# A mixture-of-experts kernel: four neighbouring weight rows to a partition, and tokens transposed by every fourth channel

## The chip, the core and the metric

The kernel runs on one core of a Trainium2 chip. The metric is the device time of one execution in microseconds (us). The engines of the core are TensorE (PE, with its weight loads shown apart as PEld), VectorE (DVE), ScalarE (ACT), GpSimd (POOL) and SyncE (SP, which here only issues transfers). Transfers run on 16 DMA engines.

## The reference

One layer of a decoder on 1024 tokens (and 16 learned ones) of 1024 channels: three mixers (a convolution, an attention with a forget gate, a state-space scan) that share one input projection, an output projection, and then a mixture of 16 experts, of which each token takes two. All data are float32. The part that the change touches:

```
    for e in range(N_EXPERTS):
        y = (jax.nn.silu(t @ w1[e]) * (t @ w3[e])) @ w2[e]
        out = out + gates[:, e:e + 1] * y.astype(jnp.float32)
```

`w1[e]` and `w3[e]` are 1024x256, `w2[e]` is 256x1024. The sum over 1024 channels in `t @ w1[e]` may be taken in any order, as long as both sides use the same one.

## The kernel before

The program has three stages: projections with convolution and scan (to about 300 us), attention and output projection with the router (to about 585 us), and the experts (585 us to the end). The first two are ordered by a scheduler with a timeline model; the experts run in an order written out by hand.

**One expert.** The router has left for each expert a list of its tokens in blocks of up to 128 (b = 0 and b = 1). POOL gathers a block by an indirect transfer (`gather`, L1210): tile `xg`, one token to a partition, 1024 channels and two gates along it. PE transposes it in two halves of 512 channels (`turn`, L1220): four transposes of 128x128 into one PSUM bank, so that channels lie on partitions. In a transpose the 128x128 piece of `xg` is the operand that PE loads (a row of PEld), and the identity matrix is streamed through. ACT copies a bank out as `xh` (L1226) and DVE writes the rest `xl` (L1227). PE multiplies by the weights with three products for each of the 8 channel blocks k (`mm3`, L280 to L282; high by high, high by low, low by high), the two matrices side by side as 512 columns. Both blocks of every expert are gathered and transposed; the products of b = 1 run only for experts with over 128 tokens. Then follow the gate (L1237 to L1240), two more transposes (L1246), the product with `w2`, a scaled copy out of PSUM (ACT L1466, or DVE L1464), and an indirect transfer that adds the rows to `h_d` in memory (`scatter`, L1263, POOL).

**Weights.** The weights of an expert come in three chunks of 1 MB: q = 0 and q = 1 hold 512 rows of `w1` and `w3` each, q = 2 is `w2`. Each has one of six buffers `eraw` (`raw_b`), 2048 words to a partition. SP issues the transfers (L1169, two for q < 2; L1173, one for q = 2). A chunk is split in two halves of 1024 words a partition (`split`, half a = 0 or 1): ACT rounds it to the high part (L1298), DVE takes the difference (L1299). As soon as half 1 of a chunk has been split, `refill` issues the next chunk of the list into the buffer that is free. Chunks of q < 2 are split at least half an expert ahead of their use.

**Before the change,** partition p takes for k = 0 to 3 the row q\*512 + k\*128 + p of `w1` and of `w3`: four runs of 1 KB each. In the buffer the four k follow one another, each with 256 words of `w1` and 256 of `w3`, so that half 0 of a chunk is k = 0 and 1 of both matrices. The transposes take 128 neighbouring channels each.

The order by hand (an expert's steps; a0, a1, b0, b1, w0, w1 are splits, t and x the transposes and their copies, f, g, u, v, s, e the products, gates and copies out):

```
ORDER = (
    "a0 f0 t00 t01 a1 ga f1 x00 s00 g0 t10 u0 x01 g1 w0 s01 v0 e00 e01 s1 x10 t11 w1 u1 b0 "
    "e10 b1 e11 x11 v1 "
).split()
```

Of the kernel before, what the change touches and what calls it, by code (L numbers as in the profile page):

```python
# [1147 lines left out]
def moe(nc, tc, p, out, dram, dr, A, bank, small, ident, mm3, rsqrt_steps, t_d, h_d, rt):  # L1148

    lst, sel, nbl = rt.lst, rt.sel, rt.nbl  # L1150
    V, S, G, PE, SY = nc.vector, nc.scalar, nc.gpsimd, nc.tensor, nc.sync
# [4 lines left out]
    raw_b = A.rot("eraw", [2048], 3, flex=False)  # L1156

    def v4(t):
        return t.rearrange("p (k f) -> p k f", k=4)

    def v2(t):
        return t.rearrange("p (k f) -> p k f", k=2)

    def load(e, q):

        raw = raw_b()
        if q < 2:
            for c, nm in ((0, "exp_w1"), (256, "exp_w3")):
                SY.dma_start(out=v4(raw)[:, :, c:c + 256],  # L1169
                             in_=p[nm][0, e, q * 512:q * 512 + 512, :].rearrange(  # L1170
                                 "(k p) f -> p k f", p=128))
        else:
            SY.dma_start(out=v2(raw), in_=p["exp_w2"][0, e].rearrange("(k p) f -> p k f", p=128))  # L1173
        return raw
# [6 lines left out]
    def load_raw(e, q):  # L1181
        return load(seq[e], q)
# [10 lines left out]
    for _ in range(3):  # L1193
        w = todo.pop(0)
# [12 lines left out]
    def gather(ix, xg=None):  # L1207
        xg = xg_b() if xg is None else xg

        G.indirect_dma_start(out=xg, out_offset=None, in_=t_d,  # L1210
                             in_offset=bass.IndirectOffsetOnAxis(ap=ix, axis=0),
                             bounds_check=NX - 1, oob_is_err=False)
        return xg

    def turn(xg, hf):

        tp = bank("xt").rearrange("p (k t) -> p k t", k=4)
        for k in range(4):
            c = (hf * 4 + k) * 128
            PE.transpose(tp[:, k, :], xg[:, c:c + 128], ident)  # L1220
        return tp

    def turned(tp, xx, hf):
# [57 lines left out]
    def shaped(t, q):  # L1281
        return v4(t) if q < 2 else v2(t)
# [51 lines left out]
    def come(b):  # L1334

        xx[0, b] = xh_b(), xl_b()
        for hf in range(2):
            turned(turn(xgs[0, b], hf), xx[0, b], hf)
        gs[0, b] = gate_of(xgs[0, b], picks(0, b))
# [87 lines left out]
    def do_turn(e, b, hf):  # L1427
        if not hf:
            xx[e, b] = xh_b(), xl_b()
        tps[e, b, hf] = turn(xgs[e, b], hf)  # L1430
# [90 lines left out]
    with tc.manual_schedule():  # L1521
# [3 lines left out]
        for e in range(NE):  # L1525
            at = e - late
            for w in ORDER + ["end"]:
                if w in steps:
                    f, d = steps[w]
# [36 lines left out]
    with tc.If(nmax > 2):  # L1566
        with tc.For_i(0, NE) as e:
            nb = nc.values_load(nbl[0:1, bass.ds(e, 1)], min_val=0, max_val=8)
            with tc.For_i(2, nb) as b:
                wt = []  # L1570
                for q in range(3):
                    raw, h, l = load(e, q), wh_b(), wl_b()
                    S.activation(out=h, in_=raw, func=AF.Copy)
                    V.tensor_tensor(out=l, in0=raw, in1=h.bitcast(F32), op=OP.subtract)
                    wt.append([shaped(h, q), shaped(l, q)])
                V.tensor_copy(out=ixd, in_=lst[:, bass.ds(e * 8 + b, 1)])
                V.tensor_copy(out=sld, in_=sel[:, bass.ds(e * 8 + b, 1), :]
                              .rearrange("p a b -> p (a b)"))
                xg, xx, yt = gather(ixd), (xh_b(), xl_b()), yt_b()
                for hf in range(2):  # L1580
                    turned(turn(xg, hf), xx, hf)
                g = gate_of(xg, sld)
                hp = bank("h")
                first(wt[:2], xx, hp)
                aa = gate_turned(turn_gate(gate(hp)))
                for hf in range(2):
                    yp = bank("y")
                    second(wt[2], aa, yp, hf)
                    V.tensor_scalar(out=yt[:, hf * 512:hf * 512 + 512], in0=yp, scalar1=g,
                                    scalar2=None, op0=OP.mult)  # L1590
                scatter(yt, ixd)
# [414 lines left out]
```

## Time and profile before

| | |
|---|---|
| time, median of 3 runs | 865.52 us (862.94 to 870.54) |
| profiled execution, its own time | 868.56 us |
| its span, first to last instruction | 866.9 us |
| PE busy | 788.9 us (91%) |
| PE weight loads busy | 641.0 us (74%) |
| DVE busy | 595.7 us (69%) |
| ACT busy | 433.9 us (50%) |
| POOL busy | 246.0 us (28%) |
| moved by DMA | 121.99 MB, 141 GB/s in the mean |

A group row of the profile reads: line, engine, operation, output <- inputs, partitions x elements, count | busy us, mean ns of one | idle time of the engine just before them and what ended it. A timeline row reads: start in us, length in us, engine, line, operation, count, and in brackets the idle time before it and who ended it. Matmuls overlap in the pipeline, so a row of eight lasts less than eight times one of them. The DMA share is the mean busy share of the 16 DMA engines.

### The profile page before, as it was taken

What the parts mean: (1) busy time and instruction counts of PE and PEld (TensorE: products, weight loads), DVE (VectorE), ACT (ScalarE), POOL (GpSimd) and SP (SyncE); (2) the same over time, 40 slices, a digit from 0 to 9 for tenths busy, and PEclk for the clock granted to TensorE, in tenths of its full rate; (3) what the DMA queues carried; (4) which work ended last, traced back from release to release, by engine and by line L of the source; (5) the groups of instructions that cost most, each with busy time, mean ns of one, the idle gap of its engine ahead of it and who ended that gap; (6) DMA issues with size and microseconds to landing.
All of it is one profiled execution on the core that took longest, in us unless ns stands there. A gap on an engine that the chain in (4) does not pass through costs nothing. (4 is left out here: it accounts for less than half of the span.)

```text
span 866.9 us, 13091 instructions
## 1 busy us (share of the span) xinstructions
PE 788.9 (91%) x4420; PEld 641.0 (74%) x4421; DVE 595.7 (69%) x1297; ACT 433.9 (50%) x785; POOL 246.0 (28%) x357
## 2 busy tenths in 40 slices
PE   3899899989999999999999999967999999897872
PEld 2899899969899965655657888855787787675662
DVE  6972599987754466666534336577788677887995
ACT  7222444524233256665564322144568565785861
POOL 4499766840001000000002010003224213323134
PEclk9998999979999999999999999988999999999996
DMA  9307131104310033021132335317699979979962
GB/s 279 84 7 140 33 104 44 43 19 117 100 53 21 13 112 133 25 74 59 64 121 55 122 122 170 122 74 241 197 292 288 276 230 271 305 248 273 326 262 107
DMA packets 89002, 121.99 MB, mean 141 GB/s; under 512 B 14843, under 2 KB 69914, under 8 KB 88928
## 3 DMA queue, kind: packets, MB, share of 16 engines
q1 hardware_dynamic: 81872, 101.98, 37.0%
q0 software_dynamic: 7056, 19.09, 8.2%
q8 instruction: 39, 0.64, 0.3%
q14 instruction: 35, 0.29, 0.1%
HBM read 101.16 MB, written 26.52 MB: 147 GB/s over the span
## 5 line engine op out<-in xcount | busy, mean ns | idle before, releaser
L280 PE MATMUL psum<-arena,arena 128*128 128x512 f32 (+4 forms) x848 | 306.3, 362 | 8.9 <-DVE arena L1461 2.4
L281 PE MATMUL psum<-arena,arena 128*128 128x512 f32 (+4 forms) x848 | 300.0, 354 | 2.0 <-DVE arena L341 2.0
L282 PE MATMUL psum<-arena,arena 128*128 128x512 f32 (+4 forms) x848 | 298.9, 353 | 0.0
L280 PEld LDWEIGHTS psum<-arena,arena 128*128 128x128 f32 x848 | 162.9, 193 | 29.9 <-issue 4.9
L281 PEld LDWEIGHTS psum<-arena,arena 128*128 128x128 f32 x848 | 163.4, 193 | 16.8 <-DVE arena L341 2.2
L282 PEld LDWEIGHTS psum<-arena,arena 128*128 128x128 f32 x848 | 162.8, 192 | 16.9 <-DVE arena L1227 0.4
L1299 DVE TENSOR_TENSOR arena<-arena,arena 128x1024 fp32r<-128x1024 f32 x96 | 113.5, 1220 | 12.6 <-ACT arena L1298 11.7
L1298 ACT ACTIVATE arena<-arena 128x1024 fp32r<-128x1024 f32 x96 | 98.6, 1071 | 0.0
L670 DVE CUSTOM_DVE_ANT_0 arena<-psum,arena 128x144 bf16<-128x144 f32 (+6 forms) x112 | 55.2, 507 | 47.5 <-PE psum L668 25.3
L725 ACT ACTIVATE arena<-psum,arena 128x512 f32<-128x512 f32 (+4 forms) x112 | 59.3, 539 | 47.9 <-PE psum L722 30.8
L728 PE MATMUL psum<-arena 128*65 128x512 f32 (+4 forms) x224 | 82.8, 455 | 0.5 <-ACT arena L725 0.5
L272 POOL TENSOR_SCALAR arena<-arena 128x1 f32<-128x1 f32 (+2 forms) x36 | 13.0, 361 | 246.9 <-ACT arena L845 72.1
L1263 POOL DMA_INDIRECT h_d<-arena x17 | 33.2, 1951 | 127.1 <-DVE arena L1227 38.9
L1226 ACT ACTIVATE arena<-psum 128x512 fp32r<-128x512 f32 x64 | 38.4, 603 | 28.4 <-PE psum L1220 28.4
L428 DVE SCALAR_TENSOR_TENSOR psum<-arena,psum 128x1024 f32<-128x1024 f32 x40 | 51.4, 1285 | 0.9
L1227 DVE TENSOR_TENSOR arena<-psum,arena 128x512 fp32r<-128x512 f32 x64 | 43.6, 684 | 12.1 <-ACT arena L1226 12.1
L665 PE MATMUL psum<-arena 128*128 128x144 f32 (+6 forms) x112 | 51.4, 483 | 0.0
L717 PE MATMUL psum<-arena 128*128 128x512 f32 (+4 forms) x112 | 47.8, 427 | 2.8 <-ACT arena L725 2.5
L438 POOL TENSOR_TENSOR arena<-arena 128x512 f32<-128x512 f32 x36 | 48.1, 1360 | 5.9 <-ACT arena L435 5.9
L1220 PE MATMUL psum<-arena 128*128 128x128 f32 x256 | 38.1, 283 | 11.8 <-DVE arena L1227 5.3
L435 ACT ACTIVATE arena<-arena 128x512 f32<-128x512 f32 x40 | 28.3, 721 | 38.0 <-POOL arena L438 24.8
L1220 PEld LDWEIGHTS psum<-arena 128*128 128x128 f32 x256 | 30.5, 144 | 22.6 <-issue 8.1
(299 smaller groups left out, 1250.6 us busy)
## 6 DMA issues: line engine op xcount, KB each, us to landing
arena<-in_exp_w_dram SPq DMA_DIRECT2D x64, 512.0 KB
arena<-in_exp_w_dram SPq DMA_DIRECT2D x16, 1024.0 KB
arena<-in_x_dram SPq DMA_DIRECT2D x16, 512.0 KB
arena<-in_w_in_dram SPq DMA_DIRECT2D x14, 512.0 KB
arena<-cr_d SPq DMA_DIRECT2D x8, 520.0 KB
arena<-in_w_out_dram SPq DMA_DIRECT2D x8, 512.0 KB
h_d<-arena SPq DMA_DIRECT2D x8, 512.0 KB
t_d<-arena SPq DMA_DIRECT2D x8, 512.0 KB
```

Of the source, the lines that this page charges most:

```text
L280: PE.matmul(out=acc, lhsT=lh[k], rhs=rh[k], start=(k == 0), stop=False)
L281: PE.matmul(out=acc, lhsT=lh[k], rhs=rl[k], start=False, stop=False)
L282: PE.matmul(out=acc, lhsT=ll[k], rhs=rh[k], start=False, stop=(k == n - 1))
L428: V.scalar_tensor_tensor(out=yc, in0=ub[:, m, w:w + NX], scalar=cwt[:, m, w:w + 1], in1=yc, op0=OP.mult, op1=OP.add)
L438: G.tensor_tensor(out=yp[:, a:a + 512], in0=yp[:, a:a + 512], in1=o, op=OP.add)
L665: PE.matmul(out=sp, lhsT=QS[:, i * 128 - 128:i * 128], rhs=KS[:, a:b], start=True, stop=not last)
L670: V.tensor_tensor_reduce(out=jk_b()[:, :b - a], in0=sp, in1=nrow[:, a:b], scale=1.0, scalar=-3.0e38, op0=OP.add, op1=OP.max, accum_out=mp[ ...
L725: S.activation(out=pt, in_=sp, func=AF.Exp, bias=ccol[:nk, j, h:h + 1])
L728: PE.matmul(out=po[:, q0 - 512 * g:512], lhsT=vt[:nk, j, h, :], rhs=pt, start=j == 0, stop=j == last, skip_group_check=True)
L1220: PE.transpose(tp[:, k, :], xg[:, c:c + 128], ident)
L1298: S.activation(out=h[:, cs], in_=raw[:, cs], func=AF.Copy)
L1299: eng.tensor_tensor(out=l[:, cs], in0=raw[:, cs], in1=h[:, cs].bitcast(F32), op=OP.subtract)
```

## The change

A partition now takes four neighbouring rows of `w1` (q\*512 + 4p to q\*512 + 4p + 3), which lie in memory as one run of 4 KB, and the same of `w3`. In the buffer the 1024 words of `w1` come first, then the 1024 of `w3`; half 0 of a chunk is `w1`, half 1 is `w3`. The moving operand of a product with block k is two runs of 256 words, 1024 words apart, where it was one run of 512. To match the new order of channels, a transpose takes every fourth channel of its half: 128 words, 16 bytes apart, where it took 128 neighbouring words. Numbers of instructions, sizes and the tiles' places are as before.

```
     def v4(t):
-        return t.rearrange("p (k f) -> p k f", k=4)
+        return t.rearrange("p (w k f) -> p k w f", w=2, k=4)
...
         if q < 2:
-            for c, nm in ((0, "exp_w1"), (256, "exp_w3")):
-                SY.dma_start(out=v4(raw)[:, :, c:c + 256],
+            for c, nm in ((0, "exp_w1"), (1024, "exp_w3")):
+                SY.dma_start(out=raw[:, c:c + 1024],
                              in_=p[nm][0, e, q * 512:q * 512 + 512, :].rearrange(
-                                 "(k p) f -> p k f", p=128))
+                                 "(p k) f -> p (k f)", p=128))
...
         for k in range(4):
-            c = (hf * 4 + k) * 128
-            PE.transpose(tp[:, k, :], xg[:, c:c + 128], ident)
+            PE.transpose(tp[:, k, :], xg[:, hf * 512 + k:hf * 512 + 512:4], ident)
         return tp
```

The first place where instructions stand otherwise is SP's list in the loop over experts, one expert's five weight transfers from its `w2` on; the branches are those of the conditional blocks (L1468 is the scatter's). Before (a wait on DVE is a wait for the split of the half that the transfer overwrites):

```order
L1173 DMA arena1_61<-in_exp_w2_dram 128x2x1024 [waits DMAHW3_49,DVE_49]
L1468 UNCONDITIONAL_BRANCH
L1169 DMA arena2_2796<-in_exp_w1_dram 128x4x256 [waits DMAHW4_49,DVE_49]
L1169 DMA arena2_2796<-in_exp_w3_dram 128x4x256 [waits DMAHW5_49]
L1169 DMA arena1_61<-in_exp_w1_dram 128x4x256 [waits DMAHW6_49,DVE_49]
L1169 DMA arena1_61<-in_exp_w3_dram 128x4x256 [waits DMAHW7_49]
```

And in the changed kernel:

```order
L1174 DMA arena1_61<-in_exp_w2_dram 128x2x1024 [waits DMAHW3_49,DVE_49]
L1170 DMA arena2_2796<-in_exp_w1_dram 128x1024 [waits DMAHW4_49,DVE_49]
L1468 UNCONDITIONAL_BRANCH
L1170 DMA arena2_2796<-in_exp_w3_dram 128x1024 [waits DMAHW5_49,DVE_49]
L1170 DMA arena1_61<-in_exp_w1_dram 128x1024 [waits DMAHW6_49,DVE_49]
L1170 DMA arena1_61<-in_exp_w3_dram 128x1024 [waits DMAHW7_49,DVE_49]
```

The transfer of `w1` waits for half 0 of its buffer alone and stands one branch earlier; that of `w3` has a wait of its own for half 1. On PE, DVE, ACT and POOL the order in the loop over experts is unchanged.

The second place is in the attention stage, where the scheduler's model of the shorter transfers has moved a split of the output projection's weights (L782) ahead of pieces of the row maxima (L670) on DVE; the same pieces of maxima (L665) stand later on PE:

```order
 L744 TENSOR_TENSOR arena_2795<-psum,arena_61 128x4x64
-L670 ISA arena_61<-psum,arena_61 128x328
-L670 ISA arena_61 128x1
-L670 ISA arena_61<-psum,arena_61 128x392
-L670 ISA arena_61 128x1
 L782 TENSOR_TENSOR arena_3626<-arena_2796,arena_3626 128x1024
```

Two pieces of the maxima that stood ahead of this split now stand behind it; what was computed there is computed all the same, a little later.

## Rows read from the trace of the kernel before

**Rows 1.** Busy time of the engines in five stretches of the expert stage (us).

```profile
core 0: us, PE busy (x) PEld busy (x) DVE busy (x) ACT busy (x) POOL busy (x), PEclk, DMA share, GB/s
592.00:712.00 120.00, 114.97 (x560) 92.75 (x559) 94.06 (x159) 80.43 (x126) 30.63 (x18) 0.97 0.82 256
712.00:745.00 33.00, 28.07 (x137) 21.15 (x136) 26.37 (x46) 23.20 (x38) 11.98 (x8) 1.00 0.98 287
745.00:785.00 40.00, 39.06 (x193) 31.23 (x192) 35.28 (x60) 29.83 (x47) 9.74 (x5) 1.00 0.86 271
785.00:801.00 16.00, 10.81 (x51) 7.89 (x50) 11.21 (x20) 10.77 (x17) 6.67 (x5) 1.00 0.96 277
801.00:836.00 35.00, 31.71 (x144) 24.32 (x144) 33.19 (x55) 26.25 (x46) 10.79 (x10) 0.95 0.84 300
```

**Rows 2.** The expert stage's weight splits and scaled copies on ACT, grouped by shape.

```profile
L1298 ACT ACTIVATE arena<-arena 128x1024 fp32r<-128x1024 f32 x91 | 93.7, 1072 | 0.0
L1466 ACT ACTIVATE arena<-psum,arena 128x512 f32<-128x512 f32 x39 | 26.9, 690 | 14.7 <-DMA h_d<-arena 14.7
```

**Rows 3.** Timelines of ACT and PE: the three places where a transfer is waited for longest.

```profile
721.02 0.69 ACT L1466 ACTIVATE arena<-psum,arena 128x512 f32<-128x512 f32 x1 [3.56 <-DMA h_d<-arena]
737.00 0.69 ACT L1466 ACTIVATE arena<-psum,arena 128x512 f32<-128x512 f32 x1 [4.42 <-DMA h_d<-arena]
795.94 0.69 ACT L1466 ACTIVATE arena<-psum,arena 128x512 f32<-128x512 f32 x1 [4.04 <-DMA h_d<-arena]
801.01 1.69 PE L1220 MATMUL psum<-arena 128*128 128x128 f32 x8 [4.78 <-DMA arena<-t_d,arena]
```

**Rows 4.** DMA traffic of 788 to 791.5 us, then of 832 to 836 us.

```profile
DMA packets 1348, 1.35 MB, mean 384 GB/s; under 512 B 34, under 2 KB 1348, under 8 KB 1348
...
DMA packets 466, 1.63 MB, mean 409 GB/s; under 512 B 67, under 2 KB 67, under 8 KB 466
```

**Rows 5.** Scatter: time to landing; and DMA queue 0 while one lands (703.4 to 713).

```profile
DMA to landing us min/median/max: 6.3/8.2/10.7
...
q0 software_dynamic: 144, 0.52, 27.6%
```

**Rows 6.** Grouped by shape, 586 us to the end: products, and loads for transposes.

```profile
L282 PE MATMUL psum<-arena,arena 128*128 128x512 f32 x264 | 105.7, 400 | 0.0
L1220 PEld LDWEIGHTS psum<-arena 128*128 128x128 f32 x256 | 30.5, 144 | 22.6 <-issue 8.1 <-DVE arena L1227 6.1 <-DVE arena L1252 2.8
```

**Rows 7.** Single lines: lengths min/median/max in ns; three on DVE, one on ACT.

```profile
L1935 DVE SCALAR_TENSOR_TENSOR arena<-arena x2: 1224/1225/1226, 205.5 to 212.3; 128x1024 f32<-128x1024 f32 x2
L1939 DVE SCALAR_TENSOR_TENSOR arena<-arena x2: 1187/1206/1225, 207.9 to 215.5; 128x1024 f32<-128x1024 f32 x2
L1948 DVE SCALAR_TENSOR_TENSOR arena<-arena x2: 2130/2148/2166, 216.6 to 231.0; 128x1024 f32<-128x1024 f32 x2
L1849 ACT ACTIVATE arena<-arena x1: 1920/1920/1920, 129.4 to 129.4; 128x2048 f32<-128x2048 f32 x1
```

**Rows 8.** Timeline of PE: eight transposes behind a product, and the product after them.

```profile
614.14 0.39 PE L282 MATMUL psum<-arena,arena 128*128 128x512 f32 x1
614.38 1.03 PE L1220 MATMUL psum<-arena 128*128 128x128 f32 x8
615.16 0.48 PE L280 MATMUL psum<-arena,arena 128*128 128x512 f32 x1
```

**Rows 9.** Timelines: transposes with two loaded columns; router products with 20 streamed columns.

```profile
388.32 0.60 PE L685 MATMUL psum<-arena 128*2 128x128 f32 x4 [0.23 <-ACT arena L686]
575.91 0.97 PEld L886 LDWEIGHTS psum<-arena 128*128 128x128 f32 x8 [0.98 <-ACT arena L883]
575.91 1.07 PE L886 MATMUL psum<-arena 128*128 128x20 f32 x8 [0.75 <-ACT arena L883]
```

**Rows 10.** The transposes in the same five stretches: PE busy, PEld busy, counts.

```profile
592.00:712.00 120.00, 19.76 (x135) 15.97 (x133) 0.97 0.82 256
712.00:745.00 33.00, 5.46 (x36) 4.01 (x36) 1.00 0.98 287
745.00:785.00 40.00, 5.87 (x43) 5.09 (x44) 1.00 0.86 271
785.00:801.00 16.00, 1.50 (x11) 0.97 (x10) 1.00 0.96 277
801.00:836.00 35.00, 5.23 (x32) 3.99 (x32) 0.95 0.84 300
```

**Rows 11.** Busy time of the engines in the attention stage, 430 to 460 us.

```profile
430.00:460.00 30.00, 29.77 (x152) 17.41 (x150) 10.35 (x30) 19.78 (x39) 0.75 (x2) 1.00 0.28 89
```

## The prediction

> **What bounds the kernel now.** The change lies in the expert stage, so I read the busy times by stretch first. From 592 to 712 us PE is busy for 114.97 of 120 us, and from 745 to 785 us for 39.06 of 40, while DVE and ACT have room [rows 1]: there, what PE is given in addition lengthens the kernel. In the other three stretches PE is idle for 4.9, 5.2 and 3.3 us. Next I ask whether weights are waited for, since the change makes their transfers shorter. They are not: ACT, which takes each chunk first, never sits idle ahead of its 91 splits [rows 2]. What ACT does wait for is the scatter of an earlier block, which must have left the buffer: 14.7 us in all [rows 2], and where it waits longest, at 721, 737 and 796 us, PE falls behind too; once PE itself waits 4.78 us for a gather [rows 3]. So transfers cost PE time at two places, 712 to 745 and 785 to 801 us, some 10 us together, through gather and scatter and not through the weights.
>
> **Weights' transfers.** Transfers of 1 KB runs alone ran at 384 GB/s, transfers of 4 KB rows (with rows from POOL's queue among them) at 409 GB/s [rows 4]. For the 2.1 MB of `w1` and `w3` of an expert that is 5.46 against 5.13 us, 0.33 us less, over 16 experts 5.3 us of DMA time. It is hidden as it is; it can only let gathers and scatters land earlier. Bounds: no gain at all, or all of the 10 us above. I take 2 us, near the lower end: a scatter needs 6.3 us to land at the least and 8.2 in the median [rows 5], and 0.33 us off each expert's traffic is small beside that.
>
> **Order of SP.** The transfer of `w1` waits for one half of its buffer instead of both, and passes a branch of SP. It starts earlier by about the time of one split (1.07 us on ACT [rows 2], a similar one on DVE). Nobody waits for it, so this gains nothing. Nothing waits longer either: that of `w3` gets the wait that both had. A first half of a chunk is now `w1` alone, so that the first product needs both halves; the splits of an expert's q < 2 chunks are done before its products start, so this is hidden.
>
> **The moving operand in two runs.** Each product reads 256 words, jumps, and reads 256 more. The trace of before has no such product. The nearest row is ACT's copy at L1849, which reads runs of 16 words and takes 1.92 us for 2048 elements, against 1.07 for 1024 in one run [rows 2, 7]: jumps at the end of such runs cost nothing. I take zero; each of three lines has 264 products, two thirds of them with `w1` and `w3` [rows 6], and if each of these 528 lost 0.01 us it would be 5 us.
>
> **The transposes.** This is the term that decides. A transpose loads 128 columns of `xg`; now they lie 16 bytes apart. What does a load cost? Eight transposes take 1.03 us; starts are 0.11 us apart [rows 8]. Two other rows say what sets these 0.11 us. Transposes with only two loaded columns and the same 128 streamed ones are 0.11 us apart too, (0.60 - 0.27)/3, so that the streaming alone takes that long [rows 9]. Products of the router with 128 loaded and only 20 streamed columns are also 0.11 us apart, (0.97 - 0.19)/7 [rows 9], so that the loading alone takes that long. (0.27 and 0.19 us are the lengths of the last one in the row.) Load and stream are level: a load lies exactly under the transpose before it, and a slower load shows in full.
>
> Would it be slower? The trace of before has no strided load of many columns. The nearest row for access in steps is on DVE: L1948 writes words 32 bytes apart and takes 2148 ns, where L1935 and L1939, the same operation on as many words in a row, take 1206 to 1225 [rows 7], a factor of 1.77. ACT's runs of 64 bytes are free, DVE's single words are not. [...] I take doubling, 0.22 us, near the factor of DVE and between the ends.
>
> [...]
>
> The sum: of four transposes behind a product, the first load has room under the product; three are longer by 0.11 us. That is 0.083 us a transpose. In the two stretches where PE is full there are 135 + 43 = 178 of them [rows 10]: 14.8 us. In the other three there are 79 [rows 10], 6.6 us; PE is idle there for 13.4 us in all, but its waits are not where the transposes are, so I count half, 3.3 us. Less 2 us for the transfers: 14.8 + 3.3 - 2 = **16.1 us slower**. The profiled execution took 868.56 us and would take 884.7. It lies 3.0 us above the median of the runs, 865.52; I forecast runs, so 865.5 + 16.1 = **881.6 us**.
>
> **The attention stage.** Maxima and a split change places. PE is busy there for 29.77 of 30 us and DVE for 10.35 [rows 11]; the same work is done by both, and PE has other products to fill in. I take zero; if PE once had to wait for the split that was put first, it would cost about that split's length, 1.2 us as for the like operations of DVE [rows 7].
>
> **Rivals.**
> - *The stepped load is as fast as before.* Then the transposes still start 0.11 us apart and what is left is the 2 us of the transfers: 863 to 866 us. [...] Against it: the factor of 1.77 on the only single-word row.
> - *Faster: gathers and scatters land early enough.* If loads are as fast as before and lighter traffic ends the waits of [rows 3], PE gains what it lost there, 4.9 + 5.2 = 10.1 us: 855.4 us. It decides where a scatter lands by some 4 us earlier than now, since that is how long ACT waits [rows 3]; against it, 0.33 us of traffic an expert is far from that.
> - *Longer packets hold up the scatter.* A scatter is 144 packets on the other queue, nine on each DMA engine [rows 5]. If an engine takes them in turn with SP's packets, each waits for 4 KB where it waited for 1 KB: at 409 GB/s over 16 engines [rows 4], 3 KB take 0.12 us, nine times 1.1 us. At the three places where ACT waits longest [rows 3] this is 3.3 us, and the kernel with fast loads and no other gain comes to 868.8 us: the 2 us are taken back and a little more. [...] No row here shows the turn.
> - *Still slower.* At DVE's 2.1 ns a word a load takes 0.27 us, 0.16 more than now; the same sum gives 0.118 us a transpose, 21.0 + 4.7 - 2 = 23.7 us, 889.2 us.
>
> **How the numbers follow.** Stepped loads slower (doubled, or up to DVE's rate): 0.50, with 872 to 892 as its own range (the lower end is a factor of 1.5 in place of 2, half of 18.1 us less 2 of gain, +7 us; the upper one the 889.2 us without all of the gain). Loads as fast, small effects of transfers in either direction, 860 to 869: 0.36. Loads as fast and the waits on transfers gone, 854 to 859: 0.14. The likeliest is the first, so the forecast is 881.6 us. The range reaches to 857 and 892: outside lie about half of the last case and 0.06 above. A measurement of this kernel tells apart about 1%. The first case is slower by over 1% in nearly all of its range, 0.47; its lowest part (0.03), and the second with 0.35, are within 1%; the third with its 0.14 and 0.01 of the second are faster, 0.15.
>
> **What would show it.** Eight transposes in a row: 1.03 us long now; over 1.6 us if loads double, the same if they don't, with the mean length of a load above its 144 ns [rows 6]. The rows between 592 and 712 us: PE stays full and the stretch with the same work gets longer. ACT's idle time ahead of L1466 tells which way the scatters went: under 14.7 us if transfers help, over it if the longer packets hold them up. A mean of the products above 400 ns [rows 6] would show the two runs of the moving operand. What would make it wrong: above all a stepped load that costs nothing.

## The result, and the profile after

The changed kernel takes 870.54 us in the median of 20 runs (865.91 to 874.24), the kernel before 866.45 us in 20 runs beside it, of which one, of 1530.23 us, was in a slow state and doesn't count. The medians lie 4.1 us apart; the ratio of the others is 1.0064, with a 95% interval of 1.0047 to 1.0081: slower by about 5.5 us (4.1 to 7.0), where 16.1 us were forecast (881.6 us). The range (857 to 892 us) holds it; "slower by over 1%" does not. The profiled execution took 868.15 us, its span is 866.5 us.

The page's busy times and SP's transfer queue, in the kernel after (engine, us, share, count; then queue, packets, MB, share of 16 engines):

```profile
PE 790.2 (91%) x4420; PEld 645.2 (74%) x4421; DVE 596.8 (69%) x1297; ACT 434.6 (50%) x785; POOL 248.0 (29%) x357
...
q1 hardware_dynamic: 57296, 101.98, 35.6%
```

PE is busy 1.3 us longer and its loads 4.2 us. SP's queue moved its 101.98 MB in 57,296 packets (81,872 before), and its share fell from 37.0% to 35.6%: the transfers did become lighter.

The spans of the two profiled executions hardly differ (866.9 and 866.5 us), and that misleads: before the expert stage, the granted clock fell in other places in the one than in the other (from 50 to 100 us it was 0.90 before and 1.00 after). So I take landmarks inside the expert stage. The program computes 32 gates on ACT (L1237). Here are all of them as a group, in the kernel before and then after (lengths in ns, first and last start in us), and after that the starts of four of them, before and after:

```profile
L1237 ACT ACTIVATE arena<-psum x32: 377/385/431, 602.1 to 834.7; 128x256 f32<-128x256 f32 x32
```

```profile
L1237 ACT ACTIVATE arena<-psum x32: 377/382/420, 595.6 to 834.3; 128x256 f32<-128x256 f32 x32
```

```profile
711.75 0.38 ACT L1237 ACTIVATE arena<-psum 128x256 f32<-128x256 f32 x1
742.22 0.41 ACT L1237 ACTIVATE arena<-psum 128x256 f32<-128x256 f32 x1
755.03 0.38 ACT L1237 ACTIVATE arena<-psum 128x256 f32<-128x256 f32 x1
815.31 0.38 ACT L1237 ACTIVATE arena<-psum 128x256 f32<-128x256 f32 x1
```

```profile
706.00 0.38 ACT L1237 ACTIVATE arena<-psum 128x256 f32<-128x256 f32 x1
739.73 0.38 ACT L1237 ACTIVATE arena<-psum 128x256 f32<-128x256 f32 x1
753.29 0.38 ACT L1237 ACTIVATE arena<-psum 128x256 f32<-128x256 f32 x1
814.98 0.38 ACT L1237 ACTIVATE arena<-psum 128x256 f32<-128x256 f32 x1
```

From the first gate to the last it is 232.6 us before and 238.7 us after. This **stretch of gates**, 6.1 us longer, is the measure that I use below for single profiles. By pieces, between the landmarks:

| piece | before | after | more |
|---|---|---|---|
| first gate to 711.75 (after: 706.00) | 109.6 | 110.4 | 0.8 |
| to 742.22 (739.73) | 30.5 | 33.7 | 3.3 |
| to 755.03 (753.29) | 12.8 | 13.6 | 0.7 |
| to 815.31 (814.98) | 60.3 | 61.7 | 1.4 |
| to the last gate | 19.4 | 19.3 | -0.1 |

In the first piece PE is full and over half of the transposes lie in it: it lost 0.8 us, where the forecast had 11. Over half of the loss lies in the second piece, where PE waits for transfers.

The rows that answer to [rows 1] (the same stretches), [rows 2] and [rows 6], in the kernel after:

```profile
592.00:712.00 120.00, 115.60 (x559) 95.20 (x559) 95.46 (x164) 81.79 (x129) 30.75 (x19) 0.97 0.75 252
712.00:745.00 33.00, 25.91 (x113) 20.00 (x112) 23.37 (x40) 19.07 (x32) 11.31 (x7) 0.90 0.92 265
785.00:801.00 16.00, 11.08 (x53) 8.66 (x51) 11.48 (x19) 9.65 (x14) 7.60 (x5) 0.92 0.88 263
```

```profile
L1466 ACT ACTIVATE arena<-psum,arena 128x512 f32<-128x512 f32 x39 | 27.0, 691 | 17.2 <-DMA h_d<-arena 17.2
L282 PE MATMUL psum<-arena,arena 128*128 128x512 f32 x264 | 106.8, 405 | 0.0
L1220 PEld LDWEIGHTS psum<-arena 128*128 128x128 f32 x256 | 38.7, 209 | 24.1 <-issue 15.3 <-DVE arena L1252 2.7 <-DVE arena L1227 2.6
```

ACT waits 17.2 us for scatters, where it waited 14.7. A load of a transpose takes 209 ns in the mean where it took 144. Of 712 to 745 us PE is busy for 25.91 us in place of 28.07, at a granted clock of 0.90 in place of 1.00. PE's two longest waits for gathers, there and at 794 us, and the row of eight transposes that answers to [rows 8]:

```profile
607.99 1.11 PE L1220 MATMUL psum<-arena 128*128 128x128 f32 x8
...
738.10 1.96 PE L1220 MATMUL psum<-arena 128*128 128x128 f32 x8 [4.57 <-DMA arena<-t_d,arena]
...
799.38 1.95 PE L1220 MATMUL psum<-arena 128*128 128x128 f32 x8 [4.74 <-DMA arena<-t_d,arena]
```

The second wait is that of [rows 3] (4.78 us before). The first is new: before, PE waited 0.41 us for this gather, and 1.57 us for DVE behind it. Eight transposes last 1.11 us in place of 1.03; the eight behind the wait last 1.96, at a granted clock of 0.50 (738.0 to 740.1 us). From 737 to 744 us, before and then after (columns as in [rows 1]):

```profile
737.00:744.00 7.00, 3.88 (x20) 2.34 (x18) 5.28 (x9) 7.00 (x12) 2.78 (x2) 1.00 0.98 293
```

```profile
737.00:744.00 7.00, 5.75 (x21) 4.72 (x21) 6.37 (x11) 3.60 (x6) 0.00 (x0) 0.51 1.03 306
```

After the wait of 4.57 us the granted clock is 0.51 of full speed in the mean of the 7 us; before, with PE idle for shorter pieces (0.41, 1.57, 0.48 and 0.66 us), it stayed at 1.00. A wait that long is not what it takes, though: in the kernel with the new buffer alone (below) PE waits 0.89 us for this gather and 1.46 us for DVE behind it, much as before, and the granted clock is 0.50 from 737 to 743.5 us.

Why does this gather come late? POOL's timeline at that place, before and then after (scatters L1263; the gather is L1210 before and L1211 after):

```profile
721.70 1.58 POOL L1263 DMA_INDIRECT h_d<-arena  x1 [4.80 <-ACT arena L1466]
728.63 1.56 POOL L1263 DMA_INDIRECT h_d<-arena  x1 [5.35 <-ACT arena L1298]
730.50 1.75 POOL L1210 DMA_INDIRECT arena<-t_d,arena  x1 [0.30 <-DVE arena L1240]
```

```profile
717.29 1.58 POOL L1263 DMA_INDIRECT h_d<-arena  x1 [3.42 <-ACT arena L1466]
726.22 2.12 POOL L1263 DMA_INDIRECT h_d<-arena  x1 [7.35 <-DMA h_d<-arena]
728.65 1.92 POOL L1211 DMA_INDIRECT arena<-t_d,arena  x1 [0.30 <-DVE arena L1227]
```

A scatter adds to `h_d`, so it waits on POOL until the one before it has landed, and the gather stands behind it. From the end of the issue of the first scatter to the gather's start it is 7.2 us before (730.50 - 723.28) and 9.8 us after (728.65 - 718.87). Before, the second scatter was released by ACT, so that the landing had come by then; after, the landing itself came last, 7.35 us behind the issue. What is late is the landing of the scatter. The DMA traffic while the packets of this scatter move, before (723.8 to 727.5 us) and then after (719.6 to 725.0 us):

```profile
DMA packets 265, 0.65 MB, mean 175 GB/s; under 512 B 15, under 2 KB 137, under 8 KB 265
...
q0 software_dynamic: 143, 0.52, 93.0%
q1 hardware_dynamic: 122, 0.12, 10.1%
```

```profile
DMA packets 411, 1.46 MB, mean 270 GB/s; under 512 B 58, under 2 KB 58, under 8 KB 410
...
q0 software_dynamic: 153, 0.50, 52.3%
q1 hardware_dynamic: 257, 0.94, 43.7%
```

The same scatter (queue 0) took 3.7 us while SP's queue (queue 1) moved 0.12 MB beside it, and 5.5 us with 0.94 MB beside it. Five scatters in the stage have 128 rows. From the trace's packets, first start to last end, they take 3.46, 4.15, 3.07, 3.68 and 3.57 us before, **3.59 us** in the mean, and 3.94, 5.99, 5.40, 5.46 and 5.17 us after, **5.19 us** in the mean. I call this mean the scatter's length below.

### The profile page after: what moved, and what is told of

The parts are those of the page before. It is cut to its first block, busy times and chain, and to the rows that moved or that the text cites. A ratio compares the mean times of both kernels' runs of the same rounds, so it can differ in the third digit from the quotient of the medians.

```text
span 866.5 us, 13118 instructions
## 1 busy us (share of the span) xinstructions
PE 790.2 (91%) x4420; PEld 645.2 (74%) x4421; DVE 596.8 (69%) x1297; ACT 434.6 (50%) x785; POOL 248.0 (29%) x357
## 3 DMA queue, kind: packets, MB, share of 16 engines
q1 hardware_dynamic: 57296, 101.98, 35.6%
## 5 line engine op out<-in xcount | busy, mean ns | idle before, releaser
L282 PE MATMUL psum<-arena,arena 128*128 128x512 f32 (+4 forms) x848 | 297.5, 352 | 0.0
L280 PEld LDWEIGHTS psum<-arena,arena 128*128 128x128 f32 x848 | 161.1, 190 | 28.7 <-issue 4.6
L281 PEld LDWEIGHTS psum<-arena,arena 128*128 128x128 f32 x848 | 161.4, 190 | 17.2 <-DVE arena L341 2.4
L282 PEld LDWEIGHTS psum<-arena,arena 128*128 128x128 f32 x848 | 160.8, 190 | 17.2 <-DVE arena L1227 0.4
L1299 DVE TENSOR_TENSOR arena<-arena,arena 128x1024 fp32r<-128x1024 f32 x96 | 113.7, 1221 | 14.0 <-ACT arena L1298 12.8
L670 DVE CUSTOM_DVE_ANT_0 arena<-psum,arena 128x144 bf16<-128x144 f32 (+6 forms) x112 | 55.1, 507 | 47.5 <-PE psum L668 25.5
L1263 POOL DMA_INDIRECT h_d<-arena x17 | 33.5, 1968 | 131.3 <-DVE arena L1227 65.9
L1220 PEld LDWEIGHTS psum<-arena 128*128 128x128 f32 x256 | 38.7, 209 | 24.1 <-issue 15.3
L1220 PE MATMUL psum<-arena 128*128 128x128 f32 x256 | 42.7, 304 | 14.9 <-DMA arena<-t_d,arena 9.3
L1227 DVE TENSOR_TENSOR arena<-psum,arena 128x512 fp32r<-128x512 f32 x64 | 43.6, 685 | 12.8 <-ACT arena L1226 12.8
L665 PE MATMUL psum<-arena 128*128 128x144 f32 (+6 forms) x112 | 51.1, 481 | 0.0
```

Of the source, the lines that this page charges most:

```text
L280: PE.matmul(out=acc, lhsT=lh[k], rhs=rh[k], start=(k == 0), stop=False)
L281: PE.matmul(out=acc, lhsT=lh[k], rhs=rl[k], start=False, stop=False)
L282: PE.matmul(out=acc, lhsT=ll[k], rhs=rh[k], start=False, stop=(k == n - 1))
L665: PE.matmul(out=sp, lhsT=QS[:, i * 128 - 128:i * 128], rhs=KS[:, a:b], start=True, stop=not last)
L670: V.tensor_tensor_reduce(out=jk_b()[:, :b - a], in0=sp, in1=nrow[:, a:b], scale=1.0, scalar=-3.0e38, op0=OP.add, op1=OP.max, accum_out=mp[ ...
L1220: PE.transpose(tp[:, k, :], xg[:, hf * 512 + k:hf * 512 + 512:4], ident)
```

## The experiments

Theory A: the stepped loads make up the loss. Theory B: the 4 KB packets hold up scatters and gathers, and PE's waits, with the lower clock behind them, make up the loss. Theory C: the buffer's new layout or the new order in the attention stage does. The first four kernels ran on one chip, beside 35 runs of the kernel before.

**The step alone.** Against the kernel before:

```
-                                 "(k p) f -> p k f", p=128))
+                                 "(p k) f -> p k f", p=128))
...
-            c = (hf * 4 + k) * 128
-            PE.transpose(tp[:, k, :], xg[:, c:c + 128], ident)
+            c = hf * 512 + k
+            PE.transpose(tp[:, k, :], xg[:, c:hf * 512 + 512:4], ident)
```

> The step alone: the transfers stay at 1 KB pieces and the buffer stays as before (k after k, w1 and w3 side by side), but a partition takes the rows 4p to 4p+3, and the transposes take every fourth channel. Theory A (the stepped loads make up the change): the ratio to before is 1.004 to 1.007 and eight transposes in a row last 1.11 us as in the changed kernel, against 1.03. Theory B (the 4 KB runs hold up gathers and scatters, and PE's waits with the lower clock behind them make up the change): 1.000 with ACT's wait for the scatter at about 15 us as before; what the transposes lose is at most 256 times 0.011 us = 2.8 us, 0.3%, and mostly covered.

Measured: ratio 0.9989 (0.9965 to 1.0014). Its transposes (lengths min/median/max in ns), and eight in a row:

```profile
L1220 PEld LDWEIGHTS psum<-arena x256: 195/210/231, 590.8 to 821.6; 128*128 128x128 f32 x128
L1220 PE MATMUL psum<-arena x256: 270/284/489, 591.0 to 821.8; 128*128 128x128 f32 x128
...
614.03 1.11 PE L1220 MATMUL psum<-arena 128*128 128x128 f32 x8
```

The loads are as long as in the changed kernel, and still the time doesn't grow. The stretch of gates is 232.0 us, ACT waits 13.7 us for scatters, the scatter's length is 3.55 us. Theory A falls.

**The 4 KB runs and the new buffer, without the step.** Against the changed kernel:

```
-            PE.transpose(tp[:, k, :], xg[:, hf * 512 + k:hf * 512 + 512:4], ident)
+            PE.transpose(tp[:, k, :], xg[:, (hf * 4 + k) * 128:(hf * 4 + k + 1) * 128], ident)
```

> The changed kernel with transposes of 128 neighbouring channels: 4 KB runs, the buffer with w1 ahead of w3, no step. The products then pair channels that don't belong together; the work is the same. Theory A: 0.997 to 1.000, eight transposes 1.03 us long. Theory B: 1.004 to 1.007, ACT's wait ahead of L1466 at 17 us or more, PE's wait for gathers at about 9 us as in the changed kernel (5 us before).

Measured: 1.0045 (1.0018 to 1.0071). ACT's wait and the loads of the transposes:

```profile
L1466 ACT ACTIVATE arena<-psum,arena 128x512 f32<-128x512 f32 x39 | 27.0, 692 | 17.4 <-DMA h_d<-arena 17.4
...
L1220 PEld LDWEIGHTS psum<-arena x256: 137/140/231, 591.2 to 824.7; 128*128 128x128 f32 x128
```

The loads are short again and the loss has stayed: stretch of gates 236.2 us, scatter's length 5.24 us. PE's waits at the transposes:

```profile
PE psum L1220 <- DVE arena L1299: 5.1, 1, 5.1
...
PE psum L1220 <- DMA arena<-t_d,arena: 3.5, 2, 3.0
```

The profile names 3.5 us of waits for gathers, not the 9 us expected, and puts 5.1 us down to a split on DVE. That is a name and no cause, as the changed kernel's second profile shows below: these 5.1 us ended with a gather too, so that 8.5 us are waits for gathers.

**The new buffer alone,** 1 KB runs and neighbouring channels (against the kernel above):

```
-                SY.dma_start(out=raw[:, c:c + 1024],
+                SY.dma_start(out=raw[:, c:c + 1024].rearrange("p (k f) -> p k f", k=4),
...
-                                 "(p k) f -> p (k f)", p=128))
+                                 "(k p) f -> p k f", p=128))
```

> The buffer alone: w1 ahead of w3, so a product's moving operand is in two runs and the transfers wait for one half each; transfers of 1 KB runs, neighbouring channels, and the attention stage in the order of the changed kernel. Theories A and B: 1.000 (0.998 to 1.002), products 400 ns in the mean. A third theory, C (the buffer's layout, or the new order in the attention stage, costs the time): 1.004 to 1.007.

Measured: 1.0002 (0.9971 to 1.0033), products of L282 405 ns, as in the changed kernel; stretch of gates 234.6 us, ACT's wait 14.5 us, scatter's length 3.96 us. Theory C falls: neither the moving operand in two runs nor the attention stage costs anything that this tells. This kernel and the one before it differ in the packets and in which rows a partition takes (which cost nothing in the step alone), and in 0.4%: the runs of the two, set beside one another, give 1.0042, by my estimate between 1.0013 and 1.0071.

**The changed kernel again.**

> The changed kernel once more, beside the three parts: 1.0047 to 1.0081 by its own interval. If effects add, its ratio less 1 is the sum of those of the step alone and of the 4 KB runs with the new buffer: by A nearly all is the step's, by B the other's. Its profile shows whether the granted clock falls in the expert stage at the same places as in its first profile (737 to 744, 798 to 805, 839 to 853 us).

Measured: 1.0048 (1.0019 to 1.0076); stretch of gates 239.1 us, scatter's length 4.98 us, ACT's wait 17.4 us. Its clock fell at 742 to 749, 803 to 810 and 844 to 858 us, the same places in the program as in the first profile (there 0.51 from 737 to 744, 0.54 from 798 to 805 and 0.52 from 839 to 853 us); but that of the new buffer alone fell there as well (737 to 744, 798 to 805 and 839 to 853 us). PE's waits at the transposes:

```profile
PE psum L1220 <- DVE arena L1299: 9.8, 2, 4.9
...
PE psum L1220 <- DMA arena<-t_d,arena: 1.5, 1, 1.5
```

By these names the waits for gathers would be gone and the loss would have stayed. But the two of 4.9 us stand ahead of the same transposes as the two of the first profile (now at 742.75 and 804.29 us), and a transpose uses nothing of a split. The trace also records at which semaphore PE stood: both times at the one that the gather sets, until its last landing at 742.62 and 804.15 us. The same holds for the 5.1 us above, and for 1.72 us ahead of the transposes at 720.6 us in the first profile, which are put down to DVE's L1252. By the semaphores PE waits 11.0 and 11.3 us for gathers in the two profiles of the changed kernel, 8.5 us in the 4 KB runs without the step and 5.2 us before.

**The changed kernel in 1 KB pieces.**

```
-                SY.dma_start(out=raw[:, c:c + 1024],
-                             in_=p[nm][0, e, q * 512:q * 512 + 512, :].rearrange(
-                                 "(p k) f -> p (k f)", p=128))
+                for h in range(2):
+                    SY.dma_start(out=raw[:, c:c + 1024].rearrange("p (a b f) -> p b a f", b=2, f=256)[:, h],
+                                 in_=p[nm][0, e, q * 512:q * 512 + 512, :].rearrange(
+                                     "(p k) f -> p k f", p=128)[:, h:4:2])
```

> The changed kernel, its steps kept, with each transfer of w1 and w3 issued as two, of rows 4p and 4p+2, and of 4p+1 and 4p+3: the same bytes to the same places in 1 KB pieces. Theory B (long packets hold up the scatters): about 1.000 (0.997 to 1.002), ACT's wait ahead of L1466 back at 14 to 15 us, transposes still 1.11 us for eight. If the loss comes from the order of the rows in memory or from the steps and the buffer together, 1.004 to 1.007 as in the changed kernel.

Measured: 1.0043 (1.0008 to 1.0078), which spoke against theory B, while the profile spoke for it: stretch of gates 232.5 us, ACT's wait 15.1 us, scatter's length 4.14 us. To settle it I ran it again on another chip, and beside it the kernel before with twice as many transfers:

> The changed kernel in 1 KB pieces (twice as many transfers) once more, beside the kernel before with twice as many transfers. Theory B (packets): the two are level within 0.2%. If packets don't matter: it stays 0.3 to 0.6% above that kernel, as the changed kernel does above the kernel before.

```
-                SY.dma_start(out=v4(raw)[:, :, c:c + 256],
+                for h in range(2):
+                    SY.dma_start(out=v4(raw)[:, h:4:2, c:c + 256],
```

> The kernel before with each transfer of w1 and w3 issued as two, of two of the four k each: the same 1 KB pieces and places, twice as many transfers. If twice as many transfers are what held the changed kernel in 1 KB pieces at 1.0043: 1.002 to 1.005. If their number is free: 0.998 to 1.002, and that kernel's loss came from its rows, steps or chance.

Measured: 0.9986 (0.9960 to 1.0012) for the changed kernel in 1 KB pieces and 0.9975 (0.9945 to 1.0004) for the kernel before with twice as many transfers. Twice as many transfers cost nothing, and the first reading didn't repeat. The two are 0.11% apart, as theory B has it. In this second profile the changed kernel in 1 KB pieces did wait for gathers (8.9 us, the longest 4.7; stretch of gates 235.5 us): a late gather was measured beside short packets too.

**The kernel before with `w2` in 1 KB pieces too** (its transfer as four, of 256 columns each).

> The kernel before, with the transfer of w2 issued as four of 256 columns each: all weights in 1 KB pieces. Theory B carried further: a scatter finds no 4 KB packets of SP's queue any more, ACT's wait ahead of L1466 falls to 11 to 14 us (14.7 before), ratio 0.996 to 1.000. If only the first two matrices' packets meet scatters, or if the time of DMA (1 KB pieces are slower: 384 against 409 GB/s) counts more: 1.000 to 1.003.

Measured: 1.0033 (1.0000 to 1.0066), and ACT's wait rose to 17.2 us. A miss. The trace shows what happened, not why: the scatter's length is 4.99 us, and 163 to 900 packets of 1 KB passed beside one scatter's 128 (37 to 403 in the kernel before and the one with the step alone). Bytes alone don't set the length either: one scatter took 5.52 us there beside 0.54 MB in 557 packets, and one of the kernel before 4.15 us beside 0.62 MB in 391. The length of SP's packets is one factor, how many pass beside a scatter's is another, and what sets the second is open. PE waits only 3.2 us for gathers in this profile.

**Three buffers for the copies out,** in the kernel before and in the changed one (`yt_b = A.rot("yt", [D], 3, flex=False)`).

> The kernel before with three buffers yt for the copies out in place of two, so that ACT's L1466 need not wait for the last scatter to land. ACT's wait ahead of L1466 (14.7 us) falls under 3 us. If PE lost its time through this buffer, 0.990 to 0.996; if it lost it through gathers that stand behind scatters on POOL's queue, 0.998 to 1.001.

> The changed kernel with three buffers yt. If the longer packets cost their time through the buffer that the scatter must leave, this kernel and the kernel before with three buffers are equal within 0.2%, but for the transposes (0 to 2.8 us); if the cost goes through POOL's queue (gathers behind scatters), the changed kernel stays 0.4 to 0.6% above it.

Measured: 1.0028 (0.9996 to 1.0060) and 1.0094 (1.0059 to 1.0129). ACT's wait is gone (0.5 and 0.0 us), and nothing is won: PE's waits for gathers became 13.0 and 17.0 us. The two stay 0.66% apart. So the cost goes through POOL's queue and not through the buffer of the copies. The four kernels measured beside the same runs of the kernel before, on one chip (this pair, `w2` in 1 KB pieces, and the first reading of the changed kernel in 1 KB pieces) all stand high; the runs of the kernel before have a mean of 864.2 us there and 865.2 to 866.1 us in the other groups of this section, so that part of 1.0028 and 1.0033 may come from these. No run shows whether it does.

**Gathers earlier,** each as soon as the block that had its buffer is transposed, in both kernels:

```
-    "a0 f0 t00 t01 a1 ga f1 x00 s00 g0 t10 u0 x01 g1 w0 s01 v0 e00 e01 s1 x10 t11 w1 u1 b0 "
-    "e10 b1 e11 x11 v1 "
+    "a0 f0 t00 t01 a1 ga f1 x00 s00 g0 t10 u0 x01 ga0 g1 w0 s01 v0 e00 e01 s1 x10 t11 w1 u1 b0 "
+    "e10 b1 e11 x11 ga1 v1 "
...
+        "ga0": (lambda e: do_gather(e, 0), 3), "ga1": (lambda e: do_gather(e, 1), 3),
```

> The kernel before with its gathers issued earlier: a block's gather as soon as the block that had its buffer is transposed (behind x01 and x11 of the order by hand), about half an expert sooner, so that it stands ahead of the scatters on POOL's queue in whose shadow it stood. Theory B2 (longer packets make scatters land later, the gathers queued behind them on POOL start later, PE waits for them and the granted clock falls after such a wait): PE's waits for gathers (5.2 us in the profile of before) nearly vanish; ratio 0.990 to 0.998. If gathers aren't what PE loses by: 0.998 to 1.002.

> The changed kernel with the same earlier gathers. Theory B2: PE's waits for gathers (9.3 us in the profile of after) go too, so that this kernel is level with the kernel before with early gathers, but for its transposes: within 0.3% of it. If the longer packets cost through something else (the copy out that waits for the buffer of a scatter, or the clock without a wait), it stays 0.4 to 0.7% above it.

Measured: 1.0029 (1.0008 to 1.0050) and 1.0038 (1.0013 to 1.0063). PE waits for no gather any more in either, and the two are 0.1% apart where the kernels without this edit are 0.5 to 0.6% apart: as expected, though their runs, set beside one another, leave room for up to 0.4% by my estimate. That the kernel before got slower by it, not faster, was not. Gathers now move while scatters do, and the scatter's length rose to 4.99 us in the one and 5.86 us in the other. ACT's wait in the second:

```profile
L1468 ACT ACTIVATE arena<-psum,arena 128x512 f32<-128x512 f32 x39 | 26.9, 691 | 20.3 <-DMA h_d<-arena 20.2
```

**Both edits.**

> The kernel before with early gathers and three buffers yt: neither a gather nor the landing of the last scatter is waited for. ACT's wait ahead of L1466 under 3 us, PE's for gathers under 2 us. Theory B2 and the buffer both: 0.985 to 0.995, the fastest of the four. If the buffer's wait was never on the path: as with early gathers alone.

> The changed kernel with early gathers and three buffers yt. With both paths from scatters to PE gone, what is left of the change is its transposes (256 times 0.011 us = 2.8 us at most) and the lighter traffic: 0 to 0.3% above the kernel before with the same two edits. If it is still 0.4% or more above, the longer packets cost by a third way.

Measured: 1.0004 (0.9977 to 1.0030) and 1.0055 (1.0037 to 1.0073), still 0.5% apart, but the waits did not go either. PE's waits (engine, line, releaser: us, times, longest), in the first and then in the second:

```profile
PE psum L1220 <- DMA arena<-t_d,arena: 4.2, 1, 4.2
```

```profile
PE psum L1220 <- DMA arena<-t_d,arena: 6.6, 1, 6.6
```

The gather stands behind a scatter once more: with three buffers the scatters are issued sooner and each waits on POOL for the landing of the one before. The one ahead of that gather waits 9.4 us in the first and 9.3 in the second.

**Without most of the traffic** (kernel before):

```
-        return load(seq[e], q)
+        return load(seq[e], q) if e < 6 or q == 2 else raw_b()
```

> The kernel before without the transfers of w1 and w3 from the seventh expert on (those products read what is left in the buffers, so their values are wrong): two thirds less weights' traffic while scatters and gathers of these experts land. If traffic on SP's queue is what makes them late: ACT's wait ahead of L1466 falls from 14.7 us to under 6 us, PE's waits for gathers under 2 us, ratio 0.985 to 0.993. If they are late by themselves (their own packets, POOL's queue): waits nearly as before, ratio 0.996 to 1.000.

Measured: 0.9937 (0.9908 to 0.9967), stretch of gates 229.3 us, scatter's length 3.34 us, and

```profile
L1466 ACT ACTIVATE arena<-psum,arena 128x512 f32<-128x512 f32 x39 | 26.9, 691 | 9.9 <-DMA h_d<-arena 9.8
```

Between the two expectations. The traffic of `w1` and `w3` from the seventh expert on costs the kernel before some 5.5 us; 9.8 us of ACT's wait are left without it, and by the semaphore PE still waits 4.8 us for the gather at 794 us.

**Other steps:** every second channel at L1223, every eighth at L1221.

> The changed kernel with two other steps in the transposes (channels and weights don't match then): every second channel (8 bytes) in the first half of a block, every eighth (32 bytes) in the second. Measured so far: step 1 word, load 140 ns, starts 109 ns apart; step 4, load 210 ns, starts 120 ns apart. If a load pays for each 16 bytes it opens anew, step 2 reads as step 1 or lies between, and step 8 as step 4 (210 and 120 ns). If it pays by the distance, step 8 reads 250 ns or more and starts 130 ns or more apart.

Measured, the loads by line (ns):

```profile
L1221 PEld LDWEIGHTS psum<-arena x128: 185/194/231, 589.6 to 825.8; 128*128 128x128 f32 x128
...
L1223 PEld LDWEIGHTS psum<-arena x128: 194/207/231, 589.0 to 822.0; 128*128 128x128 f32 x128
```

Medians of 207 ns for a step of 2 words, 194 for 8 (and 210 for 4, 140 for 1); four in a row behind a product last 0.63 us (step 2), and the four right behind these 0.61 us (step 8). Both expectations missed: it doesn't grow with the distance, and a step of 2, with two words on each 16 bytes, pays as much as 4.

Together, where gathers and buffers are as before (ratio to before; then in us from the profile the stretch of gates, its second piece, PE's waits for gathers in that piece by their semaphores, scatter's length and ACT's wait):

| kernel | packets of w1, w3 | ratio | gates | second piece | PE for gathers there | scatter | ACT |
|---|---|---|---|---|---|---|---|
| before | 1 KB | 1 | 232.6 | 30.5 | 0.4 | 3.59 | 14.7 |
| step alone | 1 KB | 0.9989 | 232.0 | 31.1 | 2.1 | 3.55 | 13.7 |
| new buffer alone | 1 KB | 1.0002 | 234.6 | 30.8 | 0.9 | 3.96 | 14.5 |
| changed, 1 KB pieces | 1 KB | 1.0043, then 0.9986 | 232.5, 235.5 | 30.2, 31.8 | 0.6, 4.3 | 4.14, 4.46 | 15.1, 14.4 |
| before, twice as many transfers | 1 KB | 0.9975 | 232.8 | 30.3 | 0.7 | 3.72 | 14.0 |
| before, `w2` in 1 KB pieces too | 1 KB | 1.0033 | 232.6 | 31.6 | 1.6 | 4.99 | 17.2 |
| 4 KB runs without step | 4 KB | 1.0045 | 236.2 | 33.0 | 3.5 | 5.24 | 17.4 |
| changed | 4 KB | 1.0064, then 1.0048 | 238.7, 239.1 | 33.7, 34.0 | 6.3, 6.3 | 5.19, 4.98 | 17.2, 17.4 |

The five ratios (of four kernels) with 1 KB packets and `w2` as before have a mean of 0.9999 (1.0005 with `w2` in 1 KB pieces as a sixth), the three with 4 KB packets one of 1.0052. The second piece tells the two kinds apart in every profile: 30.2 to 31.8 us with 1 KB packets, 33.0 to 34.0 us with 4 KB packets. No version was found that beats the kernel before by more than the measurement tells.

## Why the prediction was wrong

**What bounds the kernel.** Right: weights are not waited for, and transfers cost PE time at two places through gather and scatter. Over half of the loss arose at the first of them. The experiment without most of the traffic puts what the traffic of `w1` and `w3` costs at about 5.5 us, half of the 10 us that [rows 1] gave as the most; 3.4 us of it lie in the second piece (27.1 us).

**Weights' transfers, 2 us of gain.** Wrong in sign. The traffic did get lighter (share 35.6% in place of 37.0%), but the scatter shown took 5.5 us in place of 3.7, with 0.94 MB of SP's queue beside it in place of 0.12.

**Order of SP, moving operand in two runs, attention stage, 0 each.** Right within 0.3% (new buffer alone, 1.0002).

**The transposes, 18.1 us.** This is the step that failed: "Load and stream are level: a load lies exactly under the transpose before it, and a slower load shows in full." No run shows the doubling that the sum takes (0.22 us a load, an estimate); loads did get slower, by a factor of 1.5 (140 to 210 ns). But eight in a row went only from 1.03 to 1.11 us: 0.01 us a transpose, where 0.083 was forecast. With 257 of them in the stretches that is 2.6 us at most; the full stretch up to the gate at 711.75 us lost 0.8 us, and the kernel with the step alone loses nothing that can be measured. The error could be seen in the rows: a load of 144 ns [rows 6] with starts 0.11 us apart [rows 8] is longer than the time between two starts, so that loads already overlapped with more than one stream. From the spacing of products with few streamed columns [rows 9] I took that the load alone filled 0.11 us; a spacing that is the same in both cases doesn't tell that neither has room. How a load of 210 ns fits into starts 120 ns apart, no run here shows.

**The rival of longer packets, 868.8 us.** This is what happened, in about this size (870.5 us). Its working took one packet of SP's queue for each of the scatter's, 1.1 us a scatter; the five scatters became 1.6 us longer, with some two packets of 4 KB for each of theirs (257 to 128 in the one shown; of the 144 packets that [rows 5] counts, 16 have 4 bytes and no row). It looked only at ACT's wait (3.3 us forecast, 2.5 measured), and that wait is not what PE loses by, as the kernels with three buffers show. The path is: scatter lands later, the next scatter and the gather behind it start later on POOL, and PE waits for the gather, 4.57 us at 733 to 738 us here and 4.86 us at the same place in the second profile, with a granted clock of 0.51 from 737 to 744 us here. No run shows the turn that the rival supposes; what was measured is the count, and that isn't one to one.

**The clock** was not in the forecast. The mean granted clock of the runs is 0.958 and 0.960 for the changed kernel and 0.963 for the kernel before beside the second. But the new buffer alone had the low clock at the same three places as the changed kernel, with a ratio of 1.0002, so that the low clock behind the long wait is not shown to be part of the loss. How the 0.5% divide into the waits and the clock behind them is not settled: in the profiles the piece with the wait lost 3.3 us, the piece after it, which has most of the low clock, 0.7 us. That the path runs through the gather rests on the second piece and PE's waits in it, on the timelines, and on the pair with early gathers (0.1% apart). It is not the whole account: the changed kernel in 1 KB pieces once waited 4.3 us there and had a second piece of 31.8 us, and the pair with both edits leaves it open whether a further path adds to it.

**The chances.** 0.47 lay on "slower by over 1%" for the sake of DVE's factor of 1.77 [rows 7]. A row of one engine that writes in steps gave nearly the right length for another that reads in steps, and the wrong price, since the length was not what the path saw.

## What to carry to other kernels

Runs of 4 KB in place of 1 KB made the bulk transfers here cheaper (SP's share 35.6% in place of 37.0%) and their neighbours dearer (a scatter of 128 rows 5.19 us in place of 3.59): before lengthening the packets of a bulk transfer that is hidden anyway, look which short, awaited transfers share the DMA engines, and what is queued behind them. The slower loads cost at most what they added to the distance between starts (109 to 120 ns), not what they added to their own length (140 to 210 ns); where a row's length exceeds that distance, there is overlap that may swallow the rest. Where the name that a profile gives a wait fits nothing that the waiting instruction uses, look at which semaphore it stood. And differences under 1% need two measurements on two chips: one of mine read 1.0043 and then 0.9986.

## What the hardware showed unexpectedly

- A weight load of 128 columns at the three steps tried takes some 55 to 70 ns longer than one of neighbours: 140 ns for step 1, and 207, 210 and 194 ns for steps of 2, 4 and 8 words. The starts move from 109 to 120 ns at step 4.
- A scatter of 128 rows takes, in the mean of five, 3.3 us with hardly any traffic beside it, 3.6 to 4.5 us beside 1 KB packets of `w1` and `w3`, and 5.0 to 5.2 us beside 4 KB packets; with `w2` in four transfers of 1 KB pieces it takes 5.0 us too. Single ones differ: in the changed kernel in 1 KB pieces one took 6.48 us with 1.29 MB of SP's queue beside it.
- After a wait of PE of 4.57 us the granted clock was 0.51 from 737 to 744 us; where PE waited 0.41 and 1.57 us at this place, it stayed at 1.00, and where it waited 0.89 and 1.46 us (new buffer alone) it was 0.50 from 737 to 743.5 us.
